# The memory heads of a hybrid decoder step: two to a set of buffers, four in two rounds

## The chip, the core and the metric

The kernel runs on one core of a Trainium2 chip. The metric is the device time of one execution in microseconds; the time before is the median of three runs. A profiled execution was recorded besides. Engines are named as the profile does: PE is TensorE (PEld its weight loads), DVE VectorE, ACT ScalarE, POOL GpSimd, SP SyncE, which issues nearly all DMAs.

## What is computed

One layer of a decoder step for a prompt of 2048 positions and 32 sample rows. Three groups of heads share one input projection: a gated convolution, eight dilated-window heads (here: local heads) and four heads that attend to 256 memory tokens (here: memory heads). Their outputs, times SiLU(z), go through one output projection, a residual and a norm. The change touches only the memory heads of the prompt:

```python
def _mem_attn(qm, mk, mv):
    s = jnp.einsum('bthe,bmhe->bhtm', qm, mk, preferred_element_type=F32) * (HEAD_DIM ** -0.5)
    p = jax.nn.softmax(s, axis=-1)
    return jnp.einsum('bhtm,bmhe->bthe', p, mv.astype(F32))
...
def _finish(x, conv_y, attn_o, mem_o, z, w_out):
    lead = x.shape[:2]
    mix = jnp.concatenate([conv_y,
                           attn_o.reshape(lead + (ATTN_W,)).astype(x.dtype),
                           mem_o.reshape(lead + (MEM_W,)).astype(x.dtype)], axis=-1)
    mix = mix * jax.nn.silu(z)
    return x + mix @ w_out
```

## The kernel before

Ahead of the heads the kernel projects all inputs and writes q and k to DRAM as a high and a low float32r part (dq_hi, dq_lo, dk_hi, dk_lo). Then the heads run as units: local heads 0 to 7, memory heads 0 to 3. A unit has a part "scores" and a part "values".

**Scores.** Keys lie on the partitions (high part in 64, low part in 64), the 2048 queries along the free axis, so a score tile is keys by queries. A memory head has 256 keys, two blocks kb of 128, and the queries in two halves hf, each of two tiles of 512: eight tiles, each two matmuls (qh and ql, lines 789 and 790) into one of three PSUM banks (psQ), copied to SBUF by ScalarE (line 1024). VectorE takes a maximum over blocks of 32 keys (line 737); `finish` (lines 742 to 748) reduces it with a transpose on TensorE (line 744) to tile mc, writes that to DRAM (dmax, line 747) and loads it back spread over all partitions (tile Rm, line 748, 512 KB per half).

**Values.** GpSimd subtracts Rm from the scores (line 1041 for memory heads; 920, 921, 926, 941, 942 for local ones), ScalarE takes the exponential (1042), TensorE multiplies with the values (1046) and sums the weights with a matrix of ones (761). `finish_head` transposes the sums, inverts and spreads them (773, 775, 776, 782), VectorE scales the output tile osb (783, one buffer), and line 786 writes it to dmix in DRAM.

**Buffers.** There are two sets, of one unit each: pools keys0/keys1 (ks, kr for the regrouped k, qh, ql, partial maxima) and vals0/vals1 (Rm, S3, SS, four S tiles, v1 to v3). A local head fills all of them; a memory head uses qh, ql, a corner of ks, Rm and the four S. Unit n takes set n mod 2, so the scores of one unit run while the values of the one before do, and the next unit's loads start when the scores have left the set's keys.

**Order.** `period` interleaves scores (with priority 350), values and the loads of the next unit by due times: a generator yields the place in the period at which its next step is due. For the local heads TensorE and SP follow that order as written; from memory head 0 on the tile framework's scheduler sets the order of each engine from priorities and its own estimate. Engines run in order, so an instruction that waits holds up all behind it on its engine.

**After the heads.** When the last scores are done the keys pools close, and w_out is loaded in 16 pieces of 256 KB (woraw, four buffers, line 1148), split by ScalarE into woh (1149) and by VectorE or GpSimd into wol (1150). The output runs by row blocks of 128 positions (class Rows): the mix is loaded from dmix (mx, 1183), multiplied by z (1184), split into mh and ml (1187, 1188), and 48 matmuls of 512 columns follow (1196). Row block 16 (the samples) and the first seven of eight chunks of row blocks 0 and 1 are worked beside the last memory head; chunk 7 needs memory heads 2 and 3.

Of the kernel before, what the change touches and what calls it, by code (L numbers as in the profile page):

```python
# [8 lines left out]
F = mybir.dt.float32  # L9
R = mybir.dt.float32r  # L10
# [9 lines left out]
T = 2048  # L20
NS = 32
NR = T + NS
H = 8
HM = 4
# [250 lines left out]
def tile_step(ctx, tc, x_prompt, x_sample, mem_prompt, ck, cv, cconv, cmk, cmv, g_in, w_in, conv_w,  # L275
# [4 lines left out]
    dr = ctx.enter_context(tc.tile_pool(name="scratch", bufs=1, space=DRAM))  # L280
    psR = ctx.enter_context(tc.tile_pool(name="psR", bufs=1, space=PSUM))

    class Ring:


        def __init__(self, ids):
            self.ids, self.n = ids, 0
# [10 lines left out]
    psA = ctx.enter_context(tc.tile_pool(name="psA", bufs=1, space=PSUM))  # L298
# [117 lines left out]
    with ExitStack() as p1:  # L416
        hB = p1.enter_context(tc.tile_pool(name="rowsB", bufs=1, side="right"))
        hT["B"] = [hB.tile([128, 8, 1024], R, name="hB_" + s) for s in ("hi", "lo")]
        with ExitStack() as pv:
# [63 lines left out]
            for i in range(4):  # L483
                raw = f32(wp.tile([128, 8, 128], R, name=("whi", "wlo")[i % 2])).rearrange("p (a b) c -> p a (b c)", a=2)
                nc.sync.dma_start(raw, wcol[i * 256:(i + 1) * 256, W0["v"]:W0["v"] + 512].rearrange("(c p) n -> p c n", p=128))
                for k in range(2):
                    d = 2 * i + k
# [36 lines left out]
            steps = memory()  # L524
            for rb in range(1, 17):
                r = rows(rb)
# [177 lines left out]
    vals, keys = [None, None], [None, None]  # L704
# [5 lines left out]

    d1 = dt1.rearrange("p (r J c) -> p r J c", r=4, J=2)

    def q_load(row, turn):
        qh = keys[turn].tile([128, T], R, name="qh")
        ql = keys[turn].tile([128, T], R, name="ql")
        for g in range(2):
            nc.sync.dma_start(f32(qh[g * 64:(g + 1) * 64]), dq_hi[row:row + 64])
            nc.sync.dma_start(f32(ql[g * 64:(g + 1) * 64]), dq_lo[row:row + 64])
        return qh, ql

    parts_ = [None, None]
    dmax = [dr.tile([64, 32], F, name="dmax%d" % i) for i in range(2)]

    psQ, psT = Ring((2, 3, 4)), Ring((5,))

    class Maxima:


        def __init__(self, turn, Rm, n):
            if parts_[turn] is None:  # L730
                parts_[turn] = keys[turn].tile([128, 64, 5], F, name="mparts")
                nc.gpsimd.memset(parts_[turn], -BIG)
            self.parts, self.Rm, self.n, self.d = parts_[turn], Rm, n, dmax[turn]
# [30 lines left out]
    def finish_head(o_sb, sums, row, at):  # L764

        rx = wk.tile([128, 16, 64], F, name="rx", bufs=1)
        ls = rx[:, 0:8].rearrange("p (a b) c -> p a (b c)", a=4)
        nc.scalar.activation(ls.rearrange("p a (J b) -> p a J b", b=8),
                             sums.ps.rearrange("p x y -> p (x y)").rearrange("p (J a b) -> p a J b", a=4, b=8), AF.Copy)
        yield at  # L770
        pt = psP.tile([128, 4, 128], F, name="pp")
        for a in range(4):
            nc.tensor.transpose(pt[:, a], ls[:, a], ident)
        rl = wk.tile([128, 16], F, name="rl")
        nc.vector.reciprocal(rl.rearrange("p (a g) -> p a g", g=4), pt[:, :, 0::32])
        nc.scalar.activation(rx, rl.unsqueeze(2).to_broadcast([128, 16, 64]), AF.Copy)  # L776
        for k in range(2):
            yield at + 0.12 + 0.04 * k
            pb = psP.tile([128, 4, 128], F, name="pp")
            for i in range(4):  # L780
                c = 8 * k + 2 * i
                nc.tensor.transpose(pb[:, i], rx[:, c:c + 2].rearrange("p a e -> p (a e)"), ident)  # L782
            nc.vector.tensor_mul(o_sb[:, 4 * k:4 * k + 4], o_sb[:, 4 * k:4 * k + 4], pb)
        for g in range(2):
            dst = dmix[row:row + 64, :T].rearrange("p (r g b) -> p g r b", g=2, b=128)[:, g]
            nc.sync.dma_start(dst, o_sb[g * 64:(g + 1) * 64])
# [4 lines left out]

    def biased(S, dt, sl, ps):
        nc.vector.scalar_tensor_tensor(S, dt, sl, ps, op0=OP.mult, op1=OP.add)  # L793

    class Head:
# [5 lines left out]
        def load_qk(self):  # L801
            h, kp = self.h, keys[self.turn]
            self.ks = kp.tile([128, T], R, name="ks")
            nc.sync.dma_start(f32(self.ks[0:64]), dk_hi[h * 64:(h + 1) * 64])
            nc.sync.dma_start(f32(self.ks[64:128]), dk_lo[h * 64:(h + 1) * 64])
            self.q = q_load(h * 64, self.turn)

        def load_v(self):
            vp = vals[self.turn]
            v1 = vp.tile([128, 16, 64], F, name="v1")  # L810
            v2 = vp.tile([128, 4, 4, 64], F, name="v2")
            v3 = vp.tile([128, 16, 64], F, name="v3")
            vsrc = p_v[0, 0, :, self.h, :]
            nc.sync.dma_start(v3, vsrc.rearrange("(b r) e -> b r e", r=16))
            for r4 in range(4):
                nc.sync.dma_start(v2[:, r4], vsrc.rearrange("(j k r) e -> r k j e", r=4, k=128)[r4])
            nc.sync.dma_start(v1, vsrc.rearrange("(j k) e -> k j e", k=128))
            self.v = v1, v2, v3

        def regroup(self, d, parts):  # L820

            if self.kr is None:
                self.kr = keys[self.turn].tile([128, T], R, name="kr")
            src = f32(self.ks).rearrange("p (b a r) -> p r a b", r=4, a=d // 4)
            for r4 in parts:
                nc.scalar.activation(self.kr[:, r4 * 512:(r4 + 1) * 512].rearrange("p (a b) -> p a b", a=d // 4), src[:, r4], AF.Copy)  # L826
# [165 lines left out]
            yield from finish_head(o_sb, sums, 256 + self.h * 64, 1.21)  # L992

    class MemHead:
        def __init__(self, h, turn):
            self.h, self.turn = h, turn

        def load_qk(self):
            h = self.h
            self.q = q_load(512 + h * 64, self.turn)  # L1000
            self.mk = mk = keys[self.turn].tile([128, T], R, name="ks").rearrange("p (a b) -> p a b", b=128)[:, 0:2]
            nc.sync.dma_start(f32(mk[0:64]).rearrange("p a b -> p (a b)"), dmk_hi[h * 64:(h + 1) * 64])
            nc.sync.dma_start(f32(mk[64:128]).rearrange("p a b -> p (a b)"), dmk_lo[h * 64:(h + 1) * 64])

        def load_v(self):
            pass

        def regroup(self, d, parts):
            pass

        def scores(self):
            vp, mk, (qh, ql) = vals[self.turn], self.mk, self.q
            Rm = vp.tile([128, T], F, name="Rm")
            mx = Maxima(self.turn, Rm, 2)
            S = {}
            for hf in range(2):
                for kb in range(2):
                    S[kb, hf] = vp.tile([128, 8, 128], F, name="S", bufs=4)
                for q in range(2):
                    for kb in range(2):  # L1020
                        ps = psQ.tile([128, 4, 128], F, name="qk")
                        c = 1024 * hf + 512 * q
                        qk(ps, mk[:, kb], qh[:, c:c + 512], ql[:, c:c + 512])
                        nc.scalar.activation(S[kb, hf][:, 4 * q:4 * q + 4], ps, AF.Copy)
                    yield
                for kb in range(2):
                    mx.add(mx.parts[:, 32 * hf:32 * hf + 32, kb], S[kb, hf].rearrange("p r (x c) -> p (r x) c", c=32))
            self.S, self.Rm = S, Rm.rearrange("p (r b) -> p r b", b=128)
            for hf in range(2):
                mx.finish(hf)  # L1030
                yield

        def values(self):
            h, S, Rm = self.h, self.S, self.Rm
            po = psA.tile([128, 2, 512], F, name="acc")
            sums = Sums()
            o_sb = wk.tile([128, 8, 128], F, name="osb", bufs=1)
            o_v = o_sb.rearrange("p (a r) (J b) -> p r a J b", r=2, b=8)
            for hf in range(2):
                for kb in range(2):  # L1040
                    nc.gpsimd.tensor_sub(S[kb, hf], S[kb, hf], Rm[:, 8 * hf:8 * hf + 8])
                    nc.scalar.activation(S[kb, hf], S[kb, hf], AF.Exp)
                yield 0.25 + 0.4 * hf
                for kb in range(2):
                    for g in range(2):
                        nc.tensor.matmul(po[g * 64:(g + 1) * 64, hf], memv[:, kb, h * 64:(h + 1) * 64],
                                         S[kb, hf][:, 4 * g:4 * g + 4].rearrange("p x y -> p (x y)"),
                                         start=(kb == 0), stop=(kb == 1), skip_group_check=True)
                nc.scalar.activation(o_v[:, hf], po[:, hf].rearrange("p (J a b) -> p a J b", a=4, b=8), AF.Copy)
            for kb in range(2):  # L1050
                for r4 in range(4):
                    sums.add(r4, 0, 512, S[kb, r4 // 2][:, 4 * (r4 % 2):4 * (r4 % 2) + 4].rearrange("p x y -> p (x y)"), last=kb == 1)
            yield from finish_head(o_sb, sums, 768 + h * 64, 1.2)

    def interleave(first, second, n1, n2):

# [38 lines left out]
            x[0] -= 1.0  # L1095
            x[2] += 1.0

    units = [Head(h, h % 2) for h in range(H)] + [MemHead(h, h % 2) for h in range(HM)]
    units[0].load_qk()
    units[0].load_v()  # L1100
    units[0].regroup(16, range(4))
# [159 lines left out]
    r = Rows(15, [bp, bp])  # L1261
# [31 lines left out]
```

## Time and profile before

| | us |
|---|---|
| median of three runs (1380.0 to 1382.8) | 1382.07 |
| the profiled execution | 1383.8 |
| its span | 1381.9 |
| PE busy in it | 1244.0 (90%) |
| DVE / ACT / POOL busy | 649.9 / 436.1 / 456.4 |
| mean granted TensorE clock | 0.958 |

The times of the rows below are microseconds from the span's start. A row of an engine in order of time gives start, duration, engine, line, operation and tiles, then in brackets how long the engine sat idle before and what ended that. The memory heads stand between about 1070 and 1208 us. Buffer numbers are left out in the profile; in the order of instructions below they are kept, and lines there are those of each kernel (now up to 31 higher).

### The profile page before, as it was taken

How to read it: one execution, taken by the hardware profiler on the slowest of the kernel's cores; microseconds unless marked ns; L12 is line 12 of the kernel's file. 1: busy time of each engine (PE TensorE's matmuls, PEld its weight loads, DVE VectorE, ACT ScalarE, POOL GpSimd, SP SyncE). 2: the span in 40 equal slices, each digit the busy share in tenths (PEclk: the TensorE clock that was granted, in tenths of full speed). 3: DMA queues.
4: the chain of work that ended last, by engine and by line, in shares of the span. 5: the costliest groups of instructions: out<-in, count | busy, mean ns of one | idle time of the engine just before them, and what ended most of it. 6: DMA issues, size and time to landing. Idle time of an engine off the chain costs nothing. (4 is left out here: it accounts for less than half of the span.)

```text
span 1381.9 us, 20158 instructions
## 1 busy us (share of the span) xinstructions
PE 1244.0 (90%) x7814; PEld 1004.8 (73%) x7814; DVE 649.9 (47%) x1201; ACT 436.1 (32%) x692; POOL 456.4 (33%) x398
## 2 busy tenths in 40 slices
PE   6999999998898999999999938988888876899997
PEld 5778898977787877677887936766666432688886
DVE  4555221465556712201530537777777335554442
ACT  5433032322332010011122135555555555312111
POOL 3130010455556201001640016566666656000000
PEclk9999999999999999999999969999999998999999
DMA  6353142587887246575555358788887856675541
GB/s 228 124 152 111 41 142 89 175 266 235 256 262 245 76 104 163 156 197 167 168 161 131 83 125 190 163 175 184 170 182 162 203 129 210 183 239 188 185 153 73
DMA packets 228103, 229.56 MB, mean 166 GB/s; under 512 B 67349, under 2 KB 182281, under 8 KB 223913
## 3 DMA queue, kind: packets, MB, share of 16 engines
q1 hardware_dynamic: 216488, 207.30, 56.0%
q10 hardware_dynamic: 11520, 20.98, 4.0%
q8 instruction: 62, 1.02, 0.3%
q14 instruction: 33, 0.26, 0.1%
HBM read 171.92 MB, written 56.31 MB: 165 GB/s over the span
## 5 line engine op out<-in xcount | busy, mean ns | idle before, releaser
L359 PE MATMUL b<-hA_hi,whi 128*128 128x384 f32 (+1 forms) x576 | 191.9, 333 | 16.5 <-ACT big L607 12.1
L359 PE MATMUL b<-hA_hi,wlo 128*128 128x384 f32 (+1 forms) x576 | 189.5, 329 | 0.0
L359 PE MATMUL b<-hA_lo,whi 128*128 128x384 f32 (+1 forms) x576 | 189.2, 329 | 0.0
L351 POOL TENSOR_TENSOR wlo<-wraw,whi 128x512 fp32r<-128x512 f32 x56 | 80.2, 1450 | 295.8 <-ACT whi L350 295.0
L359 PE MATMUL b<-hB_hi,whi 128*128 128x512 f32 (+1 forms) x416 | 163.7, 393 | 8.1 <-ACT big L607 2.2
L124 POOL TENSOR_TENSOR spr<-sk,sqb 128x512 f32<-128x512 f32 (+2 forms) x110 | 121.8, 1118 | 129.5 <-DMA sk<-in_cache_win_k_dram 46.7
L359 PE MATMUL b<-hB_lo,whi 128*128 128x512 f32 (+1 forms) x416 | 163.0, 392 | 0.0
L359 PE MATMUL b<-hB_hi,wlo 128*128 128x512 f32 (+1 forms) x416 | 162.4, 390 | 0.0
L359 PEld LDWEIGHTS b<-hA_hi,whi 128*128 128x128 f32 x576 | 110.8, 192 | 23.1 <-ACT big L607 13.2
L125 DVE TENSOR_REDUCE sc<-spr 128x8 f32<-128x512 f32 (+1 forms) x160 | 88.4, 572 | 75.4 <-POOL spr L124 75.0
L793 DVE SCALAR_TENSOR_TENSOR S<-dt,b 128x128 f32<-128x128 f32 (+2 forms) x224 | 70.1, 355 | 96.4 <-PE b L790 63.2
L359 PEld LDWEIGHTS b<-hA_hi,wlo 128*128 128x128 f32 x576 | 110.6, 192 | 4.1 <-issue 3.3
L359 PEld LDWEIGHTS b<-hA_lo,whi 128*128 128x128 f32 x576 | 110.7, 192 | 2.9 <-issue 2.9
L1196 PE MATMUL b<-woh,mh 128*128 128x512 f32 x256 | 101.9, 401 | 7.7 <-ACT mh L1187 7.7
L409 POOL TENSOR_TENSOR ss<-ss,nhalf 128x1 f32<-128x1 f32 (+1 forms) x34 | 19.6, 578 | 249.5 <-DVE ss L408 249.4
L1196 PE MATMUL b<-woh,ml 128*128 128x512 f32 x256 | 101.0, 395 | 0.0
L1196 PE MATMUL b<-wol,mh 128*128 128x512 f32 x256 | 100.3, 396 | 0.0
L359 PEld LDWEIGHTS b<-hB_hi,whi 128*128 128x128 f32 x416 | 79.3, 191 | 26.3 <-issue 3.7
L926 POOL TENSOR_TENSOR S<-S,Rm 128x512 f32<-128x512 f32 x32 | 40.2, 1281 | 176.1 <-DMA Rm<-dmax 149.4
L826 ACT ACTIVATE kr<-ks 128x512 fp32r<-128x512 f32 x64 | 69.0, 1118 | 86.7 <-PE b L790 67.8
L789 PE MATMUL b<-qh,kr 128*128 128x256 f32 x256 | 74.2, 319 | 22.5 <-DMA qh<-dq_hi 21.9
L359 PEld LDWEIGHTS b<-hB_lo,whi 128*128 128x128 f32 x416 | 79.2, 190 | 19.6 <-issue 3.3
(234 smaller groups left out, 2382.1 us busy)
## 6 DMA issues: line engine op xcount, KB each, us to landing
sk<-in_cache_win_k_dram SPq DMA_DIRECT2D x72, 256.0 KB, 4.1
vq<-in_cache_win_v_dram SPq DMA_DIRECT2D x36, 512.0 KB, 4.2
wraw<-in_w_in_dram SPq DMA_DIRECT2D x48, 256.0 KB, 3.6
sqb<-dqs SPq DMA_DIRECT2D x48, 256.0 KB, 4.1
qh<-dq_hi SPq DMA_DIRECT2D x24, 512.0 KB, 11.2
ql<-dq_lo SPq DMA_DIRECT2D x24, 512.0 KB, 10.5
Rm<-dmax SPq DMA_DIRECT2D x24, 512.0 KB, 4.8
v<-out_dram SPq DMA_DIRECT2D x16, 512.0 KB, 17.9
```

The source lines that it names most:

```text
L124: E.tensor_mul(pr[:n, :width], kt, qt)
L125: nc.vector.tensor_reduce(dst, pr[:n, :width].rearrange("p (h e) -> p h e", e=64), axis=AX.X, op=OP.add)
L351: lo_eng.tensor_sub(lo[:, a:a + 4], raw, f32(hi[:, a:a + 4]))
L359: nc.tensor.matmul(ps, a(d), b(d), start=(n == 0), stop=(n == 23))
L409: nc.gpsimd.tensor_tensor(ss[:n], ss[:n], nhalf[:n], op=OP.pow)
L789: nc.tensor.matmul(out, keys, a, start=True, stop=False)
L793: nc.vector.scalar_tensor_tensor(S, dt, sl, ps, op0=OP.mult, op1=OP.add)
L826: nc.scalar.activation(self.kr[:, r4 * 512:(r4 + 1) * 512].rearrange("p (a b) -> p a b", a=d // 4), src[:, r4], AF.Copy)
L926: nc.gpsimd.tensor_sub(S3[:, r4], S3[:, r4], mr[:, r4])
L1196: nc.tensor.matmul(self.ps[k], l[:, d], r[d][:, sl], start=first and i == 0, stop=last and i == 2)
```

## The change

A pair of memory heads becomes one unit (class MemPair): pair 0 is memory heads 0 and 1 on set 0, pair 1 heads 2 and 3 on set 1. The second head of a pair takes what a local head would have used besides: its q lies in ks and kr, its Rm in S3, its eight score tiles in SS, its partial maxima in a corner of v3. The memory keys get tiles of their own (mk0, mk1), and there are four dmax in DRAM. Scores of a pair alternate between its heads step by step; `finish` now comes at the end of each half and not after both. Values of a pair run one head after the other, with due times 0.25 later for the second. The list of units has ten entries in place of twelve.

```diff
-    def q_load(row, turn):
-        qh = keys[turn].tile([128, T], R, name="qh")
-        ql = keys[turn].tile([128, T], R, name="ql")
+    def q_load(row, turn, hi="qh", lo="ql"):
+        qh = keys[turn].tile([128, T], R, name=hi)
+        ql = keys[turn].tile([128, T], R, name=lo)
...
-    dmax = [dr.tile([64, 32], F, name="dmax%d" % i) for i in range(2)]
+    dmax = [dr.tile([64, 32], F, name="dmax%d" % i) for i in range(4)]
...
+            if parts is not None:
+                self.parts, self.Rm, self.n, self.d = parts, Rm, n, dmax[2 + turn]
+                return
...
-            self.q = q_load(512 + h * 64, self.turn)
-            self.mk = mk = keys[self.turn].tile([128, T], R, name="ks").rearrange("p (a b) -> p a b", b=128)[:, 0:2]
+            self.q = q_load(512 + h * 64, self.turn, *(("ks", "kr") if self.second else ("qh", "ql")))
+            self.mk = mk = kp.tile([128, 2, 128], R, name="mk%d" % self.second)
...
+            if self.second:
+                Rm = vp.tile([128, T], F, name="S3")
+                parts = vp.tile([128, 16, 64], F, name="v3").rearrange("p a b -> p (a b)")[:, 0:128].rearrange("p (a b) -> p a b", b=2)
+                mx = Maxima(self.turn, Rm, 2, parts)
+                SS = vp.tile([128, 4, 8, 128], F, name="SS")
...
-                    S[kb, hf] = vp.tile([128, 8, 128], F, name="S", bufs=4)
+                    S[kb, hf] = SS[:, 2 * hf + kb] if self.second else vp.tile([128, 8, 128], F, name="S", bufs=4)
...
-            for hf in range(2):
                 mx.finish(hf)
                 yield
...
-                yield 0.25 + 0.4 * hf
+                yield at + 0.2 + 0.2 * hf
...
-            yield from finish_head(o_sb, sums, 768 + h * 64, 1.2)
+            yield from finish_head(o_sb, sums, 768 + h * 64, at + 0.45)
+
+    class MemPair:
+        def __init__(self, h, turn):
+            self.heads = [MemHead(h + i, turn, i) for i in range(2)]
+
+        def load_qk(self):
+            for x in self.heads:
+                x.load_qk()
...
+        def scores(self):
+            steps = [x.scores() for x in self.heads]
+            for _ in range(6):
+                for x in steps:
+                    next(x)
+                yield
+            for x in steps:
+                next(x, None)
+
+        def values(self):
+            for x in self.heads:
+                yield from x.values()
...
-    units = [Head(h, h % 2) for h in range(H)] + [MemHead(h, h % 2) for h in range(HM)]
+    units = [Head(h, h % 2) for h in range(H)] + [MemPair(0, 0), MemPair(2, 1)]
```

On SP, where the scores of local head 7 end. Before (Rm_9108 is local head 7's Rm, qh_9589 and ql_9590 the q of memory head 1, qh_9805 that of memory head 2):

```order
L717 DMA qh_9589<-dq_hi_66 64x2048
L747 DMA dmax1_6299<-mc_9466 32x32
L718 DMA ql_9590<-dq_lo_67 64x2048
L717 DMA qh_9589<-dq_hi_66 64x2048
L718 DMA ql_9590<-dq_lo_67 64x2048
L748 DMA Rm_9108<-dmax1_6299 128x1024
L747 DMA dmax1_6299<-mc_9543 32x32
L717 DMA qh_9805<-dq_hi_66 64x2048
```

And now (Rm_9110 is local head 7's Rm; qh_9619, ql_9620 are the q of memory head 2, ks_9628 and kr_9629 that of memory head 3):

```order
L717 DMA ks_9628<-dq_hi_66 64x2048 x2
L717 DMA qh_9619<-dq_hi_66 64x2048
L750 DMA dmax1_6299<-mc_9477 32x32
L718 DMA ql_9620<-dq_lo_67 64x2048
L717 DMA qh_9619<-dq_hi_66 64x2048
L718 DMA ql_9620<-dq_lo_67 64x2048
L718 DMA kr_9629<-dq_lo_67 64x2048 x2
L751 DMA Rm_9110<-dmax1_6299 128x1024
L750 DMA dmax1_6299<-mc_9565 32x32
```

Eight loads of pair 1 stand ahead of local head 7's first Rm, where four of memory head 1 stood. One period earlier pair 0's loads are eight as well, where memory head 0 had four, ahead of the loads of local head 7's values.

On GpSimd, at the end of local head 7 (SS_9110 its scores of the first window). Before (S_9510 and the rest of that name are memory head 0's):

```order
L941 TENSOR_TENSOR SS_9110<-SS_9110,Rm_9108 128x16x32
L942 TENSOR_TENSOR SS_9110<-SS_9110,Rm_9108 128x12x32
L1041 TENSOR_TENSOR S_9510<-S_9510,Rm_9509 128x1024
L1041 TENSOR_TENSOR S_9511<-S_9511,Rm_9509 128x1024
L1041 TENSOR_TENSOR S_9614<-S_9614,Rm_9509 128x1024
L1041 TENSOR_TENSOR S_9615<-S_9615,Rm_9509 128x1024
```

And now (SS_9112 is local head 7's; S_9521 to S_9680 memory head 0's, SS_9533 memory head 1's, S_9877 memory head 2's):

```order
L944 TENSOR_TENSOR SS_9112<-SS_9112,Rm_9110 128x16x32
L1045 TENSOR_TENSOR S_9521<-S_9521,Rm_9520 128x1024
L1045 TENSOR_TENSOR S_9522<-S_9522,Rm_9520 128x1024
L1045 TENSOR_TENSOR SS_9533<-SS_9533,S3_9531 128x1024 x2
L1045 TENSOR_TENSOR S_9679<-S_9679,Rm_9520 128x1024
L1045 TENSOR_TENSOR S_9680<-S_9680,Rm_9520 128x1024
L1045 TENSOR_TENSOR SS_9533<-SS_9533,S3_9531 128x1024 x2
L945 TENSOR_TENSOR SS_9112<-SS_9112,Rm_9110 128x12x32
L1045 TENSOR_TENSOR S_9877<-S_9877,Rm_9876 128x1024
L1045 TENSOR_TENSOR S_9878<-S_9878,Rm_9876 128x1024
```

Local head 7's last subtraction has moved behind all eight of pair 0.

On TensorE, at the same place. Before (acc_9496 is local head 7's output, ql_9590 memory head 1's q, qh_9805 memory head 2's):

```order
L790 MATMUL b3_9861<-ql_9590,ks_9595 128x512
L789 MATMUL b4_9908<-qh_9805,ks_9811 128x512
L790 MATMUL b4_9908<-ql_9806,ks_9811 128x512
L744 MATMUL b5_9884<-ident_75,mx_9882 32x128
L915 MATMUL acc_9496<-SS_9110,v1_9260 64x64 x11
L789 MATMUL b2_9912<-qh_9805,ks_9811 128x512
L790 MATMUL b2_9912<-ql_9806,ks_9811 128x512
L915 MATMUL acc_9496<-SS_9110,v1_9260 64x64 x5
L789 MATMUL b3_9916<-qh_9805,ks_9811 128x512
L790 MATMUL b3_9916<-ql_9806,ks_9811 128x512
L915 MATMUL acc_9496<-SS_9110,v1_9260 64x64 x12
L915 MATMUL acc_9496<-SS_9110,v1_9260 64x32 x4
```

And now (acc_9507 is local head 7's output; ks_9628 memory head 3's q, qh_9619 memory head 2's; S_9521 memory head 0's weights). The last products of local head 7 are the rows with 64x64 x28 and 64x32:

```order
L792 MATMUL b2_9910<-ks_9628,mk1_9634 128x512
L793 MATMUL b2_9910<-kr_9629,mk1_9634 128x512
L918 MATMUL acc_9507<-SS_9112,v1_9271 64x64 x28
L918 MATMUL acc_9507<-SS_9112,v1_9271 64x32 x4
L764 MATMUL b1_9508<-SS_9112,ones_80 32x480 x4
L764 MATMUL b1_9508<-SS_9112,ones_80 32x512 x4
L1050 MATMUL acc_10043<-S_9521,memv_88 64x512 x2
L1050 MATMUL acc_10043<-S_9522,memv_88 64x512 x2
L792 MATMUL b3_9902<-qh_9619,mk0_9625 128x512
L793 MATMUL b3_9902<-ql_9620,mk0_9625 128x512
L792 MATMUL b4_9906<-ks_9628,mk1_9634 128x512
L793 MATMUL b4_9906<-kr_9629,mk1_9634 128x512
```

Ten of pair 1's sixteen score tiles (b3_9902 is the first of them) stand behind local head 7's last products; before, all of memory head 1's (b3_9861 is the last) and three of memory head 2's stood ahead of those.

## Rows read from the trace of the kernel before

**Rows 1.** Chain that ended last, in order of time: start us, us, what.

```profile
1208.56 155.23 PE b L1196 x670
...
1363.79 11.01 PE b L1206 x48
```

**Rows 2.** GpSimd (POOL) in order of time, then its waits in total (us, times, longest).

```profile
1084.26 2.48 POOL L926 TENSOR_TENSOR S<-S,Rm 128x512 f32<-128x512 f32 x2 [20.04 <-DMA Rm<-dmax]
...
1106.57 0.98 POOL L942 TENSOR_TENSOR SS<-SS,Rm 128x384 f32<-128x384 f32 x1
...
1107.52 9.35 POOL L1041 TENSOR_TENSOR S<-S,Rm 128x1024 f32<-128x1024 f32 x4
...
1125.70 9.31 POOL L1041 TENSOR_TENSOR S<-S,Rm 128x1024 f32<-128x1024 f32 x4 [8.82 <-DMA Rm<-dmax]
...
1164.33 1.73 POOL L1150 TENSOR_TENSOR wol<-woraw,woh 128x512 fp32r<-128x512 f32 x1
...
1166.02 5.09 POOL L1041 TENSOR_TENSOR S<-S,Rm 128x1024 f32<-128x1024 f32 x2
...
POOL S L1041 <- DMA Rm<-dmax: 23.6, 4, 8.8
```

**Rows 3.** The chain again, where maxima travel over DRAM.

```profile
1113.41 7.84 DMA dmax<-mc
...
1135.32 0.29 DVE mc L746
...
1135.63 1.32 DMA dmax<-mc
...
1137.01 3.68 DMA Rm<-dmax
...
1140.85 2.38 POOL S L1041
```

**Rows 4.** Slices: us, five engines' busy us, PEclk, DMA share, GB/s.

```profile
810.00:815.00 5.00, 0.00 (x0) 0.00 (x0) 0.00 (x0) 2.96 (x4) 4.07 (x4) 0.50 1.01 213
...
1060.00:1065.00 5.00, 5.00 (x44) 2.90 (x40) 4.49 (x11) 2.75 (x4) 4.22 (x4) 1.00 1.02 220
...
1065.00:1070.00 5.00, 5.00 (x90) 3.91 (x82) 3.66 (x8) 0.10 (x1) 0.00 (x0) 1.00 0.13 36
...
1070.00:1075.00 5.00, 5.00 (x56) 3.22 (x54) 2.95 (x9) 1.80 (x3) 0.00 (x0) 1.00 0.71 161
...
1080.00:1085.00 5.00, 3.93 (x18) 2.32 (x16) 2.93 (x6) 1.68 (x3) 0.74 (x1) 1.00 1.02 255
...
1170.00:1175.00 5.00, 2.47 (x10) 0.70 (x10) 3.12 (x3) 3.58 (x5) 2.09 (x2) 0.63 1.02 342
```

**Rows 5.** SyncE's queue of DMA issues in order of time.

```profile
1042.68 0.49 SPq L717 DMA_DIRECT2D qh<-dq_hi  x1
...
1070.55 0.44 SPq L717 DMA_DIRECT2D qh<-dq_hi  x1
...
1075.75 0.35 SPq L748 DMA_DIRECT2D Rm<-dmax  x1
```

**Rows 6.** ScalarE (ACT) in order of time.

```profile
1108.16 0.84 ACT L943 ACTIVATE SS<-SS 128x768 f32<-128x768 f32 x1
...
1145.64 1.10 ACT L1024 ACTIVATE S<-b 128x512 f32<-128x512 f32 x2
```

**Rows 7.** TensorE: eight sums in the chain, and a slice after idle time.

```profile
1111.91 0.94 PE b L761 x8
...
1130.00:1135.00 5.00, 5.00 (x16) 2.25 (x15) 1.51 (x3) 4.30 (x7) 5.00 (x3) 0.62 0.00 0
```

**Rows 8.** The chain ahead of the output projection; the second row is SyncE's queue.

```profile
1172.53 1.22 PE b L1196 x2
...
1191.01 1.26 SPq L786 DMA_DIRECT2D dmix<-osb  x2
...
1192.36 4.48 DMA woraw<-in_w_out_dram
...
1198.14 0.48 DVE mx L1184 x2
...
1199.50 6.48 DMA mx<-dmix
...
1207.45 1.07 ACT mh L1187
```

More of the change, by code (lines that the diff above doesn't have):

```diff
@@ L721, in tile_step, with __init__ @@
     parts_ = [None, None]
-    dmax = [dr.tile([64, 32], F, name="dmax%d" % i) for i in range(2)]
+    dmax = [dr.tile([64, 32], F, name="dmax%d" % i) for i in range(4)]
     psQ, psT = Ring((2, 3, 4)), Ring((5,))
     class Maxima:
-        def __init__(self, turn, Rm, n):
+        def __init__(self, turn, Rm, n, parts=None):
+            if parts is not None:
+                self.parts, self.Rm, self.n, self.d = parts, Rm, n, dmax[2 + turn]
+                return
             if parts_[turn] is None:
@@ L994, in tile_step, with __init__ @@
     class MemHead:
-        def __init__(self, h, turn):
-            self.h, self.turn = h, turn
+        def __init__(self, h, turn, second):
+            self.h, self.turn, self.second = h, turn, second
         def load_qk(self):
-            h = self.h
-            self.q = q_load(512 + h * 64, self.turn)
-            self.mk = mk = keys[self.turn].tile([128, T], R, name="ks").rearrange("p (a b) -> p a b", b=128)[:, 0:2]
+            h, kp = self.h, keys[self.turn]
+            self.q = q_load(512 + h * 64, self.turn, *(("ks", "kr") if self.second else ("qh", "ql")))
+            self.mk = mk = kp.tile([128, 2, 128], R, name="mk%d" % self.second)
             nc.sync.dma_start(f32(mk[0:64]).rearrange("p a b -> p (a b)"), dmk_hi[h * 64:(h + 1) * 64])
             nc.sync.dma_start(f32(mk[64:128]).rearrange("p a b -> p (a b)"), dmk_lo[h * 64:(h + 1) * 64])
[L1005 to L1009, printed above, removed]
         def scores(self):
             vp, mk, (qh, ql) = vals[self.turn], self.mk, self.q
-            Rm = vp.tile([128, T], F, name="Rm")
-            mx = Maxima(self.turn, Rm, 2)
             S = {}
+            if self.second:
[3 more added lines that the diff above has]
+                SS = vp.tile([128, 4, 8, 128], F, name="SS")
+            else:
+                Rm = vp.tile([128, T], F, name="Rm")
+                mx = Maxima(self.turn, Rm, 2)
             for hf in range(2):
                 for kb in range(2):
-                    S[kb, hf] = vp.tile([128, 8, 128], F, name="S", bufs=4)
+                    S[kb, hf] = SS[:, 2 * hf + kb] if self.second else vp.tile([128, 8, 128], F, name="S", bufs=4)
                 for q in range(2):
@@ L1027, in scores @@
                     mx.add(mx.parts[:, 32 * hf:32 * hf + 32, kb], S[kb, hf].rearrange("p r (x c) -> p (r x) c", c=32))
-            self.S, self.Rm = S, Rm.rearrange("p (r b) -> p r b", b=128)
-            for hf in range(2):
                 mx.finish(hf)
                 yield
+            self.S, self.Rm = S, Rm.rearrange("p (r b) -> p r b", b=128)
         def values(self):
-            h, S, Rm = self.h, self.S, self.Rm
-            po = psA.tile([128, 2, 512], F, name="acc")
+            h, S, Rm, at = self.h, self.S, self.Rm, 0.25 * self.second
             sums = Sums()
@@ L1038, in values @@
             o_v = o_sb.rearrange("p (a r) (J b) -> p r a J b", r=2, b=8)
+            po = psA.tile([128, 2, 512], F, name="acc")
             for hf in range(2):
@@ L1052, in values, with load_v, regroup @@
                     sums.add(r4, 0, 512, S[kb, r4 // 2][:, 4 * (r4 % 2):4 * (r4 % 2) + 4].rearrange("p x y -> p (x y)"), last=kb == 1)
-            yield from finish_head(o_sb, sums, 768 + h * 64, 1.2)
+            yield from finish_head(o_sb, sums, 768 + h * 64, at + 0.45)
[5 more added lines that the diff above has]
+                x.load_qk()
+        def load_v(self):
+            pass
+        def regroup(self, d, parts):
+            pass
+        def scores(self):
[9 more added lines that the diff above has]
+                yield from x.values()
     def interleave(first, second, n1, n2):
```

## The prediction

> **What bounds the kernel now.** I read the chain of waits from its end first. From 1208.56 us on TensorE runs the output projection without a break, 670 matmuls in 155.23 us, then the 48 of the last row block [rows 1]. Nothing in that stretch waits, so the time is decided by when row block 2 of the output begins, and so by what stands ahead of it: the four memory heads, between 1070 and 1208 us. Next I read GpSimd, engine by engine in order of time. It subtracts the maxima from the scores before ScalarE takes the exponential, so every product with the values comes after it. It starts on local head 7 at 1084.26, when the maxima (tile Rm) have landed, runs through memory head 0, and then stops four times for an Rm, 23.6 us in total; its last subtraction ends at 1166.02 + 5.09 = 1171.1 [rows 2]. Each stop is the round trip of the maxima: the row maximum to DRAM (dmax), and from there to all partitions (Rm). Undisturbed that is 1.32 + 3.68 us, with waits 5.25 us from VectorE's mc (ends 1135.6) to GpSimd's start at 1140.85; behind queued q loads the dmax alone took 7.84 us [rows 3]. These stops are what the change goes for: with two heads per set of buffers, more scores can be ready ahead of GpSimd.
>
> Last I read the DMA share and rate in slices. Loads of q and k move 213 GB/s with the queue full; the slice 1080 to 1085 moves 255. Between 1065 and 1075 the queue has room, shares of 0.13 and 0.71 [rows 4]. SP issues in order, so an Rm lands after everything issued ahead of it: memory head 1's four loads begin at 1070.55, the Rm of local head 7 is issued at 1075.75 [rows 5] and GpSimd gets it at 1084.26.
>
> **The change part by part.** Arithmetic, exponentials and DMA bytes stay as they are, apart from their places. I call GpSimd's start on local head 7 T0 (now 1084.26).
>
> First, **the loads move ahead of T0.** The second head of pair 0 loads its q at once with the first (begin at 1042.68 [rows 5]), and pair 1 loads both heads when local head 7's scores end. The order on SP shows all eight loads of pair 1 ahead of Rm_9110, the Rm of local head 7; before, four stood there. That makes 4 + 4 more transfers of 512 KB ahead of it, 8 x 0.524 = 4.19 MB. At 213 GB/s they take 19.7 us. The room in the queue swallows 0.87 x 5 + 0.29 x 5 = 5.8 us. So T0 moves by +13.9 us. Bounds: at 255 GB/s 16.4 - 5.8 = +10.6; if only the first slice can be filled, +15.3. At the 342 GB/s that the output's loads reach at 1170 to 1175 [rows 4] it would be 12.3 - 5.8 = +6.5, a rival below. I take 213, since that slice holds these very loads. The wait falls on GpSimd; behind it the exponentials on ScalarE and the products on TensorE wait too.
>
> The Trainium skill (DMA: Bandwidth & Descriptors, section Specifications) gives a limit of about 358 GB/s per core from HBM. By it the 4.19 MB would take 11.7 us, T0 would move by 5.9 and the time would be some 8 us below my forecast. The trace does not bear it out for these loads, with 213 GB/s at a share of 1.01 [rows 4].
>
> Second, **GpSimd's run from T0.** Before, its end lies 1171.1 - 1084.26 = 86.85 us after T0. After, its order is: 17 of local head 7's 18 subtractions (1106.57 - 1084.26 = 22.3 us), pair 0's eight (9.35 / 4 = 2.34 each, 18.7 us), and only then local head 7's last one (0.98 us) [rows 2]. Pair 0's maxima are there by then: they are made while GpSimd works on local head 7. So two of the four stops go. But TensorE's order has local head 7's last products, which need that last subtraction and its exponential (0.84 us [rows 6]), ahead of ten of pair 1's sixteen score tiles. TensorE stands until T0 + 22.3 + 18.7 + 0.98 + 0.84 = T0 + 42.8, some 20 us, where before it had all of memory head 1's scores done in time.
>
> From there to pair 1's first Rm: 16 products, 8 sums and 4 memory products, about 3 us at full clock (eight sums take 0.94 [rows 7]); after such idle time the granted clock is 0.62 in a slice of the trace [rows 7], near the lower level of 1.2 GHz, so I take 5 us. Then eight score tiles, each with its copy on ScalarE (1.10 / 2 = 0.55 us [rows 6], with the hand-over 0.62): 5 us. Then the transposed maximum, 1 us. Then the round trip, 5.25 us. Together 16.3 us; I bound it by 12 (nothing but copies and round trip at full clock) and 20 (the first Rm behind queued w_out loads, as the 4.48 us of one show [rows 8]). GpSimd does pair 1's eight (18.7 us) and one wol piece (1.73 us): end at T0 + 42.8 + 16.3 + 20.4 = T0 + 79.5. Against 86.85 that is -7.3. One long stop replaces four short ones. With T0 later, GpSimd ends at +13.9 - 7.3 = +6.6, at 1177.7.
>
> Third, **the end.** Before, row block 2 and the rest of row block 1 begin 1208.56 - 1171.1 = 37.5 us after GpSimd's end, with 670 matmuls to go. In the new order row blocks 16, 0 and 1 are all done ahead of row block 2, so 624 are to go; the 46 between are worth 46 x 155.23 / 670 = 10.7 us. The figure to compare is thus 48.1 us. After: the weights wol of chunks 2, 4 and 6 follow GpSimd's last subtraction, and w_out pieces wait on SP for the buffers that these free; the load of row block 16's mix stands behind them. I take 10.5 us from GpSimd's end to the first output product (two pieces at 1.73 [rows 2], a w_out transfer at 4.48 and mh at 1.07 [rows 8], and 1.5 for the small mix load); now it is 1.4 (1172.53 [rows 8]). Then come 81 output products (81 x 0.232 = 18.8), 12 memory products, 8 sums and 4 transposes (4.5), and 2 us of lower clock, 25.3. Then the last head's transposes and VectorE's two multiplications, 2.3. From issue of its dmix to the product with z on VectorE 1198.14 - 1191.01 = 7.1 us, and from there to row block 2's first matmul 1208.56 - 1198.14 = 10.4 us, of which 6.48 are the load of its mix, whose buffer comes free only then [rows 8]. Sum 55.6 against 48.1: +7.5, with bounds 0 and +12, since this part has the fewest direct rows.
>
> The four early mk loads of pair 1 (64 KB each) go behind local head 1's q in the queue and ahead of nothing that waits: nothing. The maxima of the second heads need no memset. The other instructions of the local heads' periods keep their order.
>
> **Sum:** +13.9 - 7.3 + 7.5 = +14.1 us. The profiled execution took 1383.8 us (span 1381.9), 1.7 above the median; against the median 1382.07 + 14.1 = 1396 us.
>
> **The rivals.** First, *the loads are quick*: at 342 GB/s T0 moves by 6.5 only, so 1396 - 7.4 = 1389. For it speaks that the DMA engines do reach 342 GB/s in this trace, against it the slice with these loads alone. Second, *the moved loads cost nothing*, since TensorE's and SP's waits hold back less than I read: T0 stays, 1396 - 13.9 = 1382, no change. Against it stand shares of 1.01 to 1.02 on either side of the gap. Third, **faster**: GpSimd runs through both pairs without a stop. Then its end is T0 + 22.3 + 37.4 + 0.98 + 1.7 = T0 + 62.4 against 86.85, -24.5. With T0 at +13.9 and the end at +7.5 this gives 1379; with T0 as it is, 1365. It decides from the point where pair 1's maxima reach DRAM before GpSimd has done pair 0, which is what the change is named for (four in flight). The order on TensorE speaks against it: ten score tiles behind a product that waits for GpSimd.
>
> **How the numbers follow.** The forecast of 1396 (1390 to 1404) 0.55; quick loads (1386 to 1390) 0.13; no change (1379.3 to 1384.9) 0.10; faster (1362 to 1379) 0.14; still slower than 1404, if the stop of TensorE and the late w_out add up, 0.08. About 0.2%, 2.8 us, is what a measurement of this kernel can tell from no change. Faster 0.14, same 0.09, slower 0.77, where a hundredth of the no-change case falls beyond 1384.9. The range reaches down through the no-change case, 1381 to 1404, and leaves out the faster case, most of it, and the case above.
>
> **What would show it.** In the profile after, GpSimd's first subtraction of local head 7 starts near 1098 with Rm as what it waited for; TensorE is idle for about 20 us up to some 1141, released by ScalarE's exponential of SS; GpSimd has one stop of about 16 us ahead of pair 1 in place of four; the first output product comes near 1188 in place of 1172.5, and row block 2 begins past 1230. If GpSimd starts near 1085, the first step is wrong; if its stop ahead of pair 1 is under 5 us, the second; if the last 624 matmuls begin within 48 us of its end, the third.

## The result

The changed kernel takes 1415.2 us (median of four runs, 1410.3 to 1421.3) against 1381.0 before on the same chip, a ratio of 1.0243 (95% interval 1.0209 to 1.0277): slower, as forecast, but by 34 us and not by 14. The profiled execution took 1421.3 us, its span is 1419.4, 37.5 more than the span of before. Rows of before are named by their group.

The chain that ended last, from the first output product on (start us, us, what; the rows of before to set beside it are rows 1 and the first and fifth of rows 8):

```profile
1199.76 1.22 PE b L1227 x2
...
1230.24 0.78 PE b L785 x7
...
1239.26 8.21 DMA mx<-dmix
...
1252.94 148.06 PE b L1227 x622
...
1401.01 11.21 PE b L1237 x48
```

Row block 2 begins at 1252.94 with 622 matmuls to go. Before, 670 were left at 1208.56 [rows 1]; 48 of them at 0.232 us make 11.1, so the time to compare is 1219.7. TensorE again runs without a break from there, so most of the loss lies ahead of row block 2: 33.2 of the 37.5 us.

GpSimd in order of time (compare rows 2):

```profile
1101.94 2.48 POOL L929 TENSOR_TENSOR S<-S,Rm 128x512 f32<-128x512 f32 x2 [34.56 <-PE b L747]
...
1124.23 4.64 POOL L1045 TENSOR_TENSOR S<-S,Rm 128x1024 f32<-128x1024 f32 x2
...
1142.65 1.02 POOL L945 TENSOR_TENSOR SS<-SS,Rm 128x384 f32<-128x384 f32 x1
...
1162.41 4.66 POOL L1045 TENSOR_TENSOR S<-S,Rm 128x1024 f32<-128x1024 f32 x2 [18.74 <-DMA Rm<-dmax]
...
1169.26 5.10 POOL L1045 TENSOR_TENSOR SS<-SS,S 128x1024 f32<-128x1024 f32 x2 [0.96 <-DMA S<-dmax]
...
1179.39 5.60 POOL L1045 TENSOR_TENSOR SS<-SS,S 128x1024 f32<-128x1024 f32 x2
```

It starts on local head 7 17.7 us later than before, goes through pair 0 without a stop, does local head 7's last subtraction at 1142.65, and then stops once, for 18.74 us, in place of four times for 23.6 together. Its last subtraction ends at 1184.99.

SyncE's queue, and the load that the chain names ahead of GpSimd's start (compare rows 5):

```profile
1045.89 0.50 SPq L717 DMA_DIRECT2D qh<-dq_hi  x1
...
1088.91 0.36 SPq L751 DMA_DIRECT2D Rm<-dmax  x1
```

```profile
1083.70 17.02 DMA kr<-dq_lo
```

Pair 0's q was issued at 1045.89, before at 1042.68 [rows 5]: 3.2 us were lost ahead of all that the change moves. Local head 7's first Rm is issued at 1088.91 in place of 1075.75, behind eight loads, the last of which keep the DMA engines busy up to 1100.7. It lands at 1101.78, as a transpose on TensorE (L747) ends; GpSimd's row names the transpose, the forecast had named Rm.

TensorE in order of time, its waits in total (us, times, longest), and slices (us, five engines' busy us, PEclk, DMA share, GB/s; compare rows 4 and 7):

```profile
1144.60 1.92 PE L918 MATMUL acc<-SS,v 128*64 128x64 f32 x32 [19.27 <-ACT SS L946]
...
1199.76 1.22 PE L1227 MATMUL b<-woh,mh 128*128 128x512 f32 x2 [0.55 <-ACT mh L1218]
```

```profile
PE acc L918 <- ACT SS L946: 19.6, 2, 19.3
...
PE acc L1050 <- ACT osb L1053: 11.7, 3, 7.3
```

```profile
755.00:760.00 5.00, 5.00 (x17) 4.23 (x17) 0.00 (x0) 1.72 (x2) 0.00 (x0) 0.50 0.04 15
...
1125.00:1145.00 20.00, 0.73 (x20) 0.59 (x18) 0.00 (x0) 9.20 (x9) 18.67 (x9) 0.60 0.00 0
...
1145.00:1150.00 5.00, 5.00 (x48) 2.18 (x46) 0.00 (x0) 1.09 (x2) 0.00 (x0) 0.54 0.01 3
```

TensorE stands for 19.27 us until ScalarE's exponential of local head 7's last scores. The second of its waits in total was 1.3 us before: memory heads' products now stand 11.7 us for the copy of the head before them out of PSUM (TensorE's output memory) into osb. The first output product has only 0.55 us of idle time ahead of it: until then TensorE was held by the memory heads' products, transposes and waits. The first slice is the 3.2 us: TensorE ran at its lower level, 0.50, at 755 to 760 us; before, it was granted 1.00 there. Nothing that the change moves stands in that stretch, and it is left out of what follows. Such losses differ between executions of one kernel too: e8 and e11 below are the same kernel, and pair 0's first q is issued at 1041.5 in the one and at 1048.0 in the other.

### The profile page after: what moved, and what is told of

Read it like the earlier page. It is cut to its first block, busy times and chain, and to the rows that moved or that the text cites. A ratio compares the mean times of both kernels' runs of the same rounds, so it can differ in the third digit from the quotient of the medians.

```text
span 1419.4 us, 20149 instructions
## 1 busy us (share of the span) xinstructions
PE 1254.7 (88%) x7814; PEld 1011.1 (71%) x7814; DVE 646.7 (46%) x1201; ACT 438.4 (31%) x692; POOL 456.0 (32%) x398
## 5 line engine op out<-in xcount | busy, mean ns | idle before, releaser
L359 PE MATMUL b<-hA_hi,whi 128*128 128x384 f32 (+1 forms) x576 | 192.4, 334 | 14.8 <-ACT big L607 10.9
## 6 DMA issues: line engine op xcount, KB each, us to landing
v<-out_dram SPq DMA_DIRECT2D x16, 512.0 KB, 17.8
```

Of the source, the lines that this page charges most:

```text
L359: nc.tensor.matmul(ps, a(d), b(d), start=(n == 0), stop=(n == 23))
```

## The experiments

Times are told as ratios to the kernel before on the same chip. In the table, from one profiled execution each, so with such early losses in them: GpSimd's start on local head 7, the end of its last subtraction, row block 2's first matmul with 622 to go (of before and of the run with loads alone, which have 670 to go, 11.1 later than their row), and the span, all in us.

| | ratio (95%) | start | GpSimd ends | row block 2 | span |
|---|---|---|---|---|---|
| before | 1 | 1084.3 | 1171.1 | 1219.7 | 1381.9 |
| after | 1.0243 (1.0209 to 1.0277) | 1101.9 | 1185.0 | 1252.9 | 1419.4 |
| e1: order undone | 1.012 (1.007 to 1.017) | 1111.3 | 1189.6 | 1245.0 | 1407.5 |
| e2: order and loads undone | 0.997 (0.9945 to 0.9994) | 1084.8 | 1155.9 | 1216.3 | 1379.7 |
| e7: the same again | 0.9946 (0.9915 to 0.9977) | 1083.6 | 1153.6 | 1221.3 | 1384.8 |
| e3: output tiles of their own | 1.0139 (1.0075 to 1.0204) | 1099.1 | 1184.0 | 1244.9 | 1405.8 |
| e4: w_out without GpSimd | 1.0232 (1.0182 to 1.0282) | 1102.4 | 1186.1 | 1255.7 | 1419.0 |
| e5: before, loads alone | 1.015 (1.0105 to 1.0195) | 1097.8 | 1194.6 | 1242.7 | 1408.5 |
| e8: e2 and e3 together | 0.9896 (0.9847 to 0.9945) | 1081.1 | 1153.1 | 1209.5 | 1370.3 |
| e11: the same again | 0.9934 (0.9911 to 0.9957) | 1087.9 | 1158.0 | 1219.0 | 1379.8 |

**e5, the loads alone, in the kernel before.**

```diff
             self.q = q_load(512 + h * 64, self.turn)
-            self.mk = mk = keys[self.turn].tile([128, T], R, name="ks").rearrange("p (a b) -> p a b", b=128)[:, 0:2]
+            if h < 2:
+                for name, src in (("ks", dq_hi), ("kr", dq_lo)):
+                    x = keys[self.turn].tile([128, T], R, name=name)
+                    for g in range(2):
+                        nc.sync.dma_start(f32(x[g * 64:(g + 1) * 64]), src[512 + h * 64:576 + h * 64])
+            self.mk = mk = keys[self.turn].tile([128, 2, 128], R, name="mk")
```

> The kernel before, with the change's extra loads and nothing else of it: memory heads 0 and 1 load a second q of the same size into ks and kr, which nobody reads, and their memory keys get a tile of their own. As in the changed kernel eight loads stand ahead of local head 7's first Rm, and four more one period earlier; GpSimd's order stays that of before. First term of the prediction: GpSimd's start on local head 7 moves by 14 us (bounds 10.6 and 15.3), from 1084 to 1098, and as nothing on its way is made up, the kernel takes 14 us more than before, a ratio of 1.010. If the four stops of GpSimd behind it take part of it up: 1.003 to 1.007. If the loads are hidden: 1.000.

GpSimd in order of time, and a slice:

```profile
1097.75 2.49 POOL L926 TENSOR_TENSOR S<-S,Rm 128x512 f32<-128x512 f32 x2 [34.41 <-DMA Rm<-dmax]
...
1109.58 2.48 POOL L926 TENSOR_TENSOR S<-S,Rm 128x512 f32<-128x512 f32 x2 [4.97 <-DMA Rm<-dmax]
```

```profile
1080.00:1090.00 10.00, 2.10 (x8) 1.16 (x6) 2.56 (x3) 1.07 (x2) 0.00 (x0) 0.74 1.01 213
```

The start moves by 13.5 us (forecast 13.9), and the loads move 213 GB/s, as in rows 4. The Trainium skill (DMA: Bandwidth & Descriptors, section Specifications) gives a limit of about 358 GB/s; by that as their rate the start would move by 5.9 us, an estimate, and the slice shows these loads well under that limit. But the kernel loses more than the start does: 1.5%, 20.8 us. The second Rm of local head 7 is late as well (the stop of 4.97), and the stops behind it add up to 29.1 us in place of 23.6. Nothing on the way makes the delay up.

**e1, GpSimd's order undone in the changed kernel** (e2 undoes the order of the loads as well).

```diff
-    streams = []
+    streams, HP = [], [0]
...
-            place = next(x[1], None)
+            with tc.high_priority(HP[0]):
+                place = next(x[1], None)
...
+    HP[0] = 400
     periods(H, len(units) - 1, 6)
```

> The changed kernel, with one thing undone: the values of local head 7 get a higher priority, so that its last subtraction stands ahead of pair 0's eight on GpSimd and its last products no longer wait for them. All eight loads of pair 1 still stand ahead of local head 7's first Rm. Theory A (GpSimd's path, as in the prediction, its second term): GpSimd still starts on local head 7 near 1102 us; TensorE's stop of 19 us ahead of pair 1 and most of GpSimd's stop of 18.7 us go; GpSimd ends near 1170 in place of 1185, and the kernel takes 1415 - 15 = 1400. Theory B (the outputs of the heads pass one after the other through the one tile osb): from local head 7's dmix to the last memory head's dmix it took 69 us before and 71 after, whatever GpSimd did, so the time follows local head 7's dmix (1161 after, 1122 before); that moves to about 1138, and the kernel to 1392. If the stop does not matter: 1415.

GpSimd in order of time, two rows of the chain, TensorE's wait for osb, and its first output product:

```profile
1111.30 2.48 POOL L929 TENSOR_TENSOR S<-S,Rm 128x512 f32<-128x512 f32 x2 [38.46 <-DMA Rm<-dmax]
...
1133.46 1.04 POOL L945 TENSOR_TENSOR SS<-SS,Rm 128x384 f32<-128x384 f32 x1
...
1134.42 4.75 POOL L1045 TENSOR_TENSOR S<-S,Rm 128x1024 f32<-128x1024 f32 x2
...
1165.53 4.70 POOL L1045 TENSOR_TENSOR S<-S,Rm 128x1024 f32<-128x1024 f32 x2 [12.48 <-DVE mx L745]
```

```profile
1089.49 17.35 DMA dmax<-mc
...
1245.00 144.36 PE b L1229 x622
```

```profile
PE acc L1050 <- ACT osb L1053: 1.0, 2, 0.7
```

```profile
1192.81 0.74 PE L1229 MATMUL b<-woh,mh 128*128 128x512 f32 x2 [1.84 <-ACT mh L1220]
```

Local head 7's last subtraction stands ahead of pair 0 again, TensorE's stop of 19 us is gone, and the kernel gains 17 us. Not by the route that theory A told: GpSimd starts 9.4 us later still. Of these, 5.5 us are there already when pair 0's q is issued (1051.37 in place of 1045.89). The rest comes with the loads: the priority lifts them too, so local head 7's first dmax now stands behind all eight (17.35 us for 4 KB). GpSimd also stops for 12.48 us ahead of pair 1. Theory B missed as well: local head 7's dmix stays near 1156, not 1138.

From GpSimd's start to the end of the span it takes 296.2 us; in the changed kernel 317.5, before 297.6. I put the difference of 21 us down to the stop of TensorE; counted from pair 0's q, which leaves the later start in, it is 17. Only 4.8 us of it show on GpSimd (78.3 against 83.1 from start to last subtraction). The rest shows behind GpSimd's end: the first output product comes 3.3 us after it (1192.81) and not 14.8, and the wait for osb falls from 11.7 us to 1.0.

**e2, the loads undone besides.** In place of the priority, SyncE follows the order as written for one period more, which puts pair 1's loads behind both Rm and brings the same order on GpSimd.

```diff
-    periods(H, len(units) - 1, 6)
+    with tc.manual_schedule(engines={mybir.EngineType.SP}):
+        periods(H, len(units) - 1, 6)
```

> As the run before this, and besides all loads of pair 1 stand behind both Rm of local head 7 in SyncE's queue; of the change's extra loads only the four of pair 0's second head are left ahead of it. First term of the prediction (each transfer of 512 KB ahead of that Rm costs GpSimd's start 2.46 us, less the room in the queue): GpSimd starts on local head 7 at 1084 to 1090 in place of 1102, and the kernel is 12 to 16 us faster than the run before this. If the loads were not what held the Rm, the start stays near 1102 and the two runs are alike. Pair 1's scores come later for it; if they come too late, GpSimd stops ahead of pair 1 and the gain is lost.

> The run with all loads of pair 1 behind local head 7's Rm, once more, as the measure for the next one on the same chip: within 3 us of the kernel before, GpSimd's last subtraction some 15 us earlier than before and yet row block 2 of the output no earlier.

GpSimd in e2, then the chain in e7, and in e7 one row each of VectorE, GpSimd and TensorE:

```profile
1084.75 2.48 POOL L929 TENSOR_TENSOR S<-S,Rm 128x512 f32<-128x512 f32 x2 [16.79 <-DMA Rm<-dmax]
...
1114.77 4.71 POOL L1045 TENSOR_TENSOR S<-S,Rm 128x1024 f32<-128x1024 f32 x2 [6.66 <-DMA Rm<-dmax]
...
1124.85 4.74 POOL L1045 TENSOR_TENSOR S<-S,Rm 128x1024 f32<-128x1024 f32 x2 [0.71 <-DMA Rm<-dmax]
...
1150.74 5.14 POOL L1045 TENSOR_TENSOR SS<-SS,S 128x1024 f32<-128x1024 f32 x2
```

```profile
1168.78 1.01 PE b L1228 x2
...
1194.37 5.74 issue
...
1208.36 7.49 DMA mx<-dmix
...
1221.32 145.31 PE b L1228 x622
```

```profile
1141.01 13.14 DVE L1182 TENSOR_TENSOR wol<-woraw,woh 128x512 fp32r<-128x512 f32 x1
...
1148.97 4.63 POOL L1045 TENSOR_TENSOR SS<-SS,S 128x1024 f32<-128x1024 f32 x2
...
1156.72 1.97 PE L785 MATMUL b<-ident,rx 128*128 128x128 f32 x8 [11.27 <-ACT rx L779]
```

The start is back at 1084.75, and GpSimd runs from 1124.85 to its last subtraction without a stop for an Rm: this is what the change is named for. GpSimd ends 15 to 18 us earlier than before. Yet row block 2 begins at 1216 to 1221, where 1219.7 is the time to compare, and the kernel gains 0.3 to 0.5%. From GpSimd's end to row block 2 it now takes 60 to 68 us and not 48.6. The first output product comes 8.1 us after GpSimd's end in e2 and 15.2 in e7, though TensorE has no stop of 19 us in either. In e7 one piece of wol on VectorE takes 13.14 us and ends half a microsecond after GpSimd's last subtraction (1153.59). The sums of a memory head are inverted behind that piece on VectorE, and TensorE stands for 11.27 us. In e2 no piece takes over 2.83 us. Further on in the chain of e7, 5.74 us of "issue" stand ahead of the last head's output, whose transposes are placed behind early output products; and the load of row block 2's mix takes 7.49 us behind it. GpSimd's end no longer sets row block 2 by itself.

**e3 and e4, two suspects of the end in the changed kernel.** e3:

```diff
-            o_sb = wk.tile([128, 8, 128], F, name="osb", bufs=1)
+            o_sb = vals[self.turn].tile([128, 4, 4, 64] if self.second else [128, 16, 64], F, name="v2" if self.second else "v1")
+            o_sb = o_sb.rearrange("p a (x y) b -> p (a x) (y b)", y=2) if self.second else o_sb.rearrange("p (a x) b -> p a (x b)", x=2)
```

> The changed kernel, in which each memory head scales its output in a tile of its own (v1 or v2 of its set, which are free then), so that a head's copy from PSUM no longer waits until the dmix of the head before has landed. Loads and GpSimd's order stay. Theory B (one osb): the 71 us from local head 7's dmix to the last head's dmix shrink to under 60, and the kernel to about 1400 to 1405. Theory A and theory C (the pieces of w_out): GpSimd still ends near 1185, the first output product still comes near 1200, and the time stays within 3 us of 1415.

e4:

```diff
-                (nc.gpsimd if (2 * d + k) % 4 < 1 else nc.vector).tensor_sub(wol[d][:, sl], raw, f32(woh[d][:, sl]))
+                nc.vector.tensor_sub(wol[d][:, sl], raw, f32(woh[d][:, sl]))
```

> The changed kernel, in which VectorE splits all pieces of w_out, none GpSimd, so that no woraw buffer waits for GpSimd's last subtractions. Theory C (third term of the prediction: the first output product waits for pieces of w_out that GpSimd holds): the first output product comes near 1188 to 1190 in place of 1199.8, row block 2 some 8 to 10 us earlier, the kernel near 1406. Theory B (one osb): the last head's dmix stays near 1232 and the time within 3 us of 1415, as the early row blocks only wait longer for chunk 7.

With tiles of their own the kernel gains 1%, with GpSimd where it was (1184.0) and row block 2 8 us earlier. That speaks for theory B in part, but the edit also moved TensorE's order: in e3 the first output product stands behind more of the heads' work, at 1208.99, so tile and order are not told apart. e4 shows no effect. In its chain the first output product comes even later than in the changed kernel:

```profile
1202.29 0.73 PE b L1227 x2
```

So the w_out pieces that GpSimd held did not set the end by themselves, though the chain of the changed kernel runs through loads of w_out; VectorE, which then had 16 pieces and not 12 (19.8 us in place of 15.6), may have taken back what GpSimd gave. The time between local head 7's dmix and the last one, on which theory B was built, was not a constant: 71 us after, 69 in e1, 65 in e3, 75 in e4, 81 in e2.

**e8, both together, and the kernel before with the same edits.** e8 is e2 with e3's tiles. The controls are the kernel before with SyncE's order as written for the period of memory head 0 (e6), with output tiles in v1 (e9), and with both (e10).

> The changed kernel with SyncE's order as written (pair 1's loads behind local head 7's Rm) and with an output tile of its own for each memory head (v1 or v2 of its set). In its order TensorE finishes all four heads ahead of all but two of the output products, so 814 of these then follow without a wait. Theory B (one osb holds the heads' outputs up): the last dmix comes near 1175 to 1180 in place of 1197, and with 814 products at 0.232 us (189 us) and 11 us for the end the kernel takes 1370 to 1378, less than before. Theory A (only GpSimd's path counts): as the run without tiles of their own, 1384.

> The kernel before, with one thing taken from the run with all loads of pair 1 behind: SyncE follows the order as written through the period of memory head 0, so that the four loads of memory head 1 stand behind both Rm of local head 7. No pairs. If the order on SyncE's queue and not the pairs gave that run its 18 us over the run with the order of GpSimd alone, the kernel before gains too: GpSimd starts on local head 7 near 1080 in place of 1084 and the time falls by 4 us or more. If memory head 1's later q only widens GpSimd's later stops, the time stays within 2 us of before.

> The kernel before, with an output tile of its own (v1 of its set) for each memory head and nothing else. If the one tile osb holds up the heads there too, the last dmix comes earlier than 1191 and the time falls by some 8 to 14 us, as it did with the changed kernel. If GpSimd's four stops set the pace before, the heads come apart in time, one waits little for the other's dmix, and the time stays within 4 us of before.

> The kernel before with both edits of the fastest run so far, SyncE's order as written and output tiles of their own, but no pairs. If these two edits give that run its 15 us, and the pairs nothing, this one takes 0.990 of before too. If they pay only with pairs, since the four stops of GpSimd for an Rm remain here: 0.997 to 1.003, with GpSimd's last subtraction at about 1171.

> The pairs with SyncE's order as written and output tiles of their own, once more, as the measure for the other two on the same chip: 0.990 of before, GpSimd's last subtraction near 1153.

GpSimd and the chain in e8, and row block 2 in e11; then e6, GpSimd's start and its waits in total:

```profile
1081.08 2.48 POOL L929 TENSOR_TENSOR S<-S,Rm 128x512 f32<-128x512 f32 x2 [17.98 <-DMA Rm<-dmax]
...
1110.62 4.71 POOL L1046 TENSOR_TENSOR S<-S,Rm 128x1024 f32<-128x1024 f32 x2 [6.19 <-DMA Rm<-dmax]
...
1147.54 5.55 POOL L1046 TENSOR_TENSOR SS<-SS,S 128x1024 f32<-128x1024 f32 x2
```

```profile
1175.78 30.46 PE b L1229 x133
...
1209.52 142.65 PE b L1229 x622
...
1352.16 11.01 PE b L1239 x48
```

```profile
1219.01 142.64 PE b L1229 x622
```

```profile
1074.36 2.52 POOL L926 TENSOR_TENSOR S<-S,Rm 128x512 f32<-128x512 f32 x2 [12.82 <-DMA Rm<-dmax]
```

```profile
POOL S L1041 <- DMA Rm<-dmax: 36.0, 5, 11.0
```

e8 beats both kernels: 0.9896, and 0.9934 (0.9911 to 0.9957) when it was run again (e11). All heads are done ahead of all but two of the output products, and row block 2 follows at 1209.52 after a wait of 3 us. In e11 it follows at 1219.01, 9.5 us later, of which 6.5 were lost before pair 0's q. The controls gain nothing: 0.9996 (0.997 to 1.0022) for e6, 0.9986 (0.9964 to 1.0008) for e9, 1.0003 (0.9979 to 1.0027) for e10. In e9 TensorE's order moved as in e8, with the first output product at 1185.10, behind all heads, and without pairs that gained nothing. In e6 GpSimd starts on local head 7 10 us earlier, and its waits for an Rm of the memory heads grow from 23.6 to 36.0 us: with one head to a set the round trips take the gain back. So the pairs do pay, but only with the loads put back: 0.3 to 0.5% with that alone, 0.7 to 1.0% with the tiles besides. On the same chip e8's executions (1370.9 to 1374.5) all lie under e7's (1375.7 to 1386.8). What e8 gains over e7 need not lie in the tile: the wait for osb was already down to 1.4 us in e7, and TensorE's order changed with it.

## Why the prediction was right in sign and wrong in size

**The loads ahead of T0: right.** T0 came at 1101.94; without the 3.2 us that were lost earlier that is +14.5 against a forecast of +13.9, and e5, with the loads alone, gave +13.5. The rivals of quick loads (+6.5) and of loads that cost nothing fall by the same numbers.

**GpSimd's run: right in shape, 3.6 us short.** The order argument held: TensorE idle for 19.27 us (forecast some 20), released by the exponential of SS; one long stop in place of four, 17.8 us from the end of that exponential to pair 1's first Rm (forecast 16.3, bound 20). In that stretch the products and sums that I priced at 5 us took 7.1, since I had read the order's counts as the trace's, which are twice as high. The run took 83.1 us against 79.5: 1.4 up to the end of the stop, 1.0 from a second wait, for the Rm of the pair's second head, the rest from subtractions that took 2.5 to 2.8 us each beside VectorE's wol, not 2.34.

**The end: the step that failed.** Forecast 55.6 us from GpSimd's end to row block 2, bounds 48.1 and 60.1; measured 68.0. Leg by leg: 14.8 to the first output product (forecast 10.5); 30.5 from there to the last head's transposes (forecast 25.3: the 12 memory products of the order are 24 matmuls in the trace, three times 1.87 us, and the 8 sums are 16); 22.7 to row block 2 (forecast 19.8; the load of its mix took 8.21 and not 6.48). Against the 48.1 of before that is +19.9 in place of +7.5, and with T0 and GpSimd's run it makes up the miss; the last 4 us of the profiled span came behind row block 2 (166.5 against 162.7).

A cost that I had not seen stands behind this. I took TensorE's stop as a cost to GpSimd alone and priced it there (one long stop for four short ones, -7.3). But all that TensorE had to do in those 19 us, local head 7's products and the values of pair 0, was put off too. Much of it fell into the stretch behind GpSimd, where the heads' outputs went through one osb, and held TensorE until 0.55 us before the first output product. e1 supports this: without the stop the first leg is 3.3 us and the whole 55.4. That this is near my 55.6 is luck, since the legs are not (3.3, 30.3 and 21.9). It is not the whole cause: e2 and e7 have no such stop either, and first legs of 8.1 and 15.2 us, the latter with VectorE's long piece of wol in it. How the first leg divides between TensorE's late work and VectorE beside GpSimd is open. The prediction had named such a case, slower than 1404 if the stop of TensorE and the late w_out add up, but gave it 0.08 and left it out of the range.

**The rival "faster" fell where the prediction put its decision, and again behind it.** In the changed kernel pair 1's maxima came late, with the stop of 18.74 us. In e2 they were there in time, and from start to last subtraction GpSimd took 71.1 us, 15.7 less than before. I expected such a gain to reach the end. Little of it did (0.3 to 0.5%). The heads' outputs, wol on VectorE and the placing of the last head's transposes stand in those chains; which of them took it up is not told apart. e8 and e11 brought more of it through (0.7 to 1.0%).

What stays open: e3 and e8 changed the output tile and with it TensorE's order, and no run here tells the two apart. In e2 and e7 the same kernel had row block 2 at 1216 and 1221, with e7's long piece of wol ahead of it; the stretch behind GpSimd varies from run to run.

## What to carry to other kernels

A stop of an engine that works in order is to be priced twice: by what it holds up on the engine that you watch, and by its own work that then falls due later, in a stretch that may be full. When a change lets an engine run ahead, ask for the next thing that is single (here an output tile, and the place of the last head's transposes among the output products) before the gain is booked. And loads that are made earlier for a later unit cost the small transfers of the unit in hand; their place in the queue has to be chosen together with the buffers.

## What was new about the hardware

- A transfer of 4 KB (dmax) took 1.32 us alone [rows 3], 7.84 behind four loads of 512 KB, and 17.35 behind eight in e1.
- VectorE and GpSimd were slower side by side than alone. GpSimd's 128x1024 subtractions took 2.33 us each with VectorE off wol and 2.5 to 2.8 beside it (rows above). VectorE waited far longer: a piece of wol took 0.69 us while GpSimd was idle, 1.71 beside its work (both below), and in e7 13.14, while GpSimd went through its subtractions at 2.3 us each. The changed kernel:

```profile
1167.14 1.71 DVE L1181 TENSOR_TENSOR wol<-woraw,woh 128x512 fp32r<-128x512 f32 x1 [1.48 <-ACT woh L1180]
...
1193.75 0.69 DVE L1181 TENSOR_TENSOR wol<-woraw,woh 128x512 fp32r<-128x512 f32 x1 [1.31 <-ACT woh L1180]
```

- During its stop TensorE, idle from about 1125 to 1144.6, was granted 0.60 in 1125 to 1145, with 0.50, the lower of its two levels, in the last 15 us of it; it still had 0.54 in 1145 to 1150, back at work, and 1.00 in 1150 to 1155. Its mean clock over the span was 0.941, before 0.958. TensorE was busy 1254.7 us against 1244.0 for the same 7814 matmuls, so 10.7 of the 37.5 us show as longer busy time and 26.8 as idle time.
